# Gate and up projections with the weights as stationary operand, and x normalised before it is transposed

## The chip, the cores and the metric

The kernel runs on one core of a Trainium2 chip. The metric is the device time of one execution in microseconds; the median of several runs is compared. Work is shared by TensorE (PE, matrix products, with PEld for the load of its stationary operand), VectorE (DVE), ScalarE (ACT), GpSimd (POOL) and SyncE (SP), whose queue issues all of the DMAs. The engines run independently and wait for each other through semaphores; each works through its own instructions in order.

## The reference

Two layers of a trunk over 256 tokens of width 1024, in float32. Each layer is a feed-forward block (FFN 1), a mixer and another feed-forward block (FFN 2):

```
def rmsnorm(x, g):
    y = x * lax.rsqrt(jnp.mean(x * x, axis=-1, keepdims=True) + EPS)
    return y * g

def swiglu(h, w_gate, w_up, w_down):            # 1024 -> 2816 -> 1024
    return (jax.nn.silu(h @ w_gate) * (h @ w_up)) @ w_down

for i in range(2):
    x = x + 0.5 * swiglu(rmsnorm(x, ffn1_norm[i]), ...)
    h = rmsnorm(x, mix_norm[i])
    q_s, k_s, v_s, q_m = split(h @ w_in[i])      # 1024 -> 2560
    # layer 0: chunked attention with a relative bias; layer 1: differential attention with
    # rotary positions; both: 4 heads of attention into mem (256 rows, keys and values of its own)
    x = x + concat([o_s, o_m]) @ w_out[i]
    x = x + 0.5 * swiglu(rmsnorm(x, ffn2_norm[i]), ...)
```

## The kernel before

**Number format.** Each operand of a dense product is split into two float32r parts, hi (the value cast) and lo (the rest), and each K tile of 128 rows is three products: hi by hi, hi by lo, lo by hi (`dense`, L375; L382, L385 and L388 are the three). ScalarE makes hi and VectorE makes lo, for activations and for all of the weights.

**Weight stream.** Weights come as chunks of 1 MB ([128, 2048] float32). `loader` issues their DMAs on SP's queue as soon as one of 3 raw buffers is free; `split_hi` (L301) and `split_lo` (L313) split a chunk in four lots of 512 columns into one of 4 pairs of hi and lo buffers. A pair is free again when the last product of its chunk has been issued (`c.uses`). At the start, the loads of x stand between the first chunks on the same queue.

**FFN.** A group is 256 columns of gate and the same 256 of up, two chunks; there are 11 groups (`ffn`, L477). The stationary operand is a K tile of x^T for one block of 128 tokens, the moving operand a [128, 512] piece of weights, gate and up side by side. Per group: 2 token blocks x 8 K tiles x 3 = 48 products of 512 columns into two PSUM banks, one per block. `evac` takes silu of gate (L488) and multiplies by up (L491), for each block. The result h has tokens on its partitions; the down projection needs it with features there, so four transposes per group (L502, issued by `turn`, L395) put h^T into a bank `htp`, and ScalarE and VectorE split it from there (L506, L508). Then the down projection (11 chunks x 8 uses x 3 = 264 products per FFN) adds up in four banks; its last three chunks are worked through block by block and half by half, so that the first token block's x is complete while products of the second still run.

**Normalisation.** `finish` adds a finished half (512 columns of a token block) to x. `prep_half` (L416) at once transposes the raw x (four transposes), multiplies by the norm's gain per column, and splits the result into xh and xl. Squares and the power that gives 1/rms per token (`square`, `prep_rstd`) come later and beside it; 1/rms is applied where the products leave PSUM: as `scale` of the silu and of the multiplication in `evac`, and in the mixer's `head_norm`, `v_evac` and `vq_evac`.

**Order.** The program's order is made by a planner (`Flow`) when the program is built: dense products follow one after another, and the work of the other engines, and transposes, are placed between them by an estimate of when their operands are there, with a fixed cost for each kind (T_MM = 0.216 us for a product of 512 columns). Splits of weights are idle work: they are added when ScalarE's or VectorE's planned queue is under 0.4 us long. At the end of a mixer `table_hint` issues a dummy silu, which loads ScalarE's table for the FFN that follows.

The mixer of layer 0 starts with the products for the memory's keys and values, that of layer 1 with its projection at once (`proj`, L834), block 0 ahead of block 1.

Of the kernel before, what the change touches and what calls it, by code (L numbers as in the profile page):

```python
# [12 lines left out]
F32 = mybir.dt.float32  # L13
F32R = mybir.dt.float32r
# [6 lines left out]
P = 128  # L21
# [19 lines left out]
T_MM = 0.216  # L41
T_TR = 0.107
# [100 lines left out]
def kernel(  # L143
# [44 lines left out]
    load_x(0, 0)  # L188

# [61 lines left out]
    dma_free = [2.3]  # L251
# [10 lines left out]
    def loader():  # L262
        for i, c in enumerate(chunks):
# [4 lines left out]
            for j, (dst, src) in enumerate(c.parts):  # L268
                nc.sync.dma_start(out=dst(c.raw), in_=src)
                dma_free[0] += 2.9 / len(c.parts)  # L270
                if j == 1 and i < 2:
                    c.early = dma_free[0] + LAT
                    if i:
                        load_x(1, 1)
                        dma_free[0] += 0.7
# [61 lines left out]
    def plan_ffn(l, nm, wg, wu, wd):  # L337
        gu = []
        for g in range(NG):
            ids = []  # L340
            for c in range(2):
# [3 lines left out]
                ids.append(add_chunk([q for ab in zip(a, b) for q in ab]))  # L345
# [29 lines left out]
    def dense(ps, xh, xl, ready, c, need, sl, start, stop):  # L375
        """One K tile of a product: three passes over the parts of both operands."""
# [29 lines left out]
    class Xt:  # L406
        def __init__(self):
            self.h = [xtp.tile([P, KT, P], F32R, tag=f"xh{tb}", name=f"xh{tb}") for tb in range(2)]
            self.l = [xtp.tile([P, KT, P], F32R, tag=f"xl{tb}", name=f"xl{tb}") for tb in range(2)]
            self.ss = [sm.tile([P, 2], F32, tag="xss", name="xss", bufs=4) for _ in range(2)]  # L410
            self.r = [sm.tile([P, 1], F32, tag="xr", name="xr", bufs=4) for _ in range(2)]
            self.t = [[None] * KT for _ in range(2)]
            self.rt = [None, None]
            self.done = [0, 0]

    def prep_half(xt, tb, hf, gc, wait=0.0):  # L416
# [12 lines left out]
        nc.scalar.copy(out=xt.h[tb][:, ks, :], in_=y)  # L429
        yield flow.act(512)  # L430
        nc.vector.tensor_sub(xt.l[tb][:, ks, :], y, xt.h[tb].bitcast(F32)[:, ks, :])
# [4 lines left out]
        flow.spawn(square(xt, tb, hf, flow.now + wait))  # L436

    def square(xt, tb, hf, t):
        yield t
        nc.scalar.activation(junk, xs[tb][:, hf * 512:(hf + 1) * 512], AF.Square,  # L440
                             accum_out=xt.ss[tb][:, hf:hf + 1])
        yield flow.act(512, 0.1)
        xt.done[tb] += 1
        if xt.done[tb] == 2:
            yield from prep_rstd(xt, tb)

    def prep_rstd(xt, tb):
        s = small([P, 1], "sst")
        nc.vector.tensor_add(s, xt.ss[tb][:, 0:1], xt.ss[tb][:, 1:2])
        flow.dve(1, 0.15)  # L450
        yield from rsqrt(xt.r[tb], s, 1, 1.0 / D)
        xt.rt[tb] = flow.now
# [6 lines left out]
    def finish(acc, tb, xt, gc, half):  # L459
        for hf in range(2):  # L460
# [12 lines left out]
            else:  # L473
                yield from prep_half(xt, tb, hf, gc)

# [1 line left out]
    def ffn(l, nm, xt, gc_next):  # L477
# [3 lines left out]
        def evac(g, ps, end):  # L481
            hs = []
            for tb in range(2):
                yield lambda: end[tb] is not None and xt.rt[tb] is not None
# [3 lines left out]
                nc.scalar.activation(sil, ps[tb][:, 0:256], AF.Silu, scale=xt.r[tb])  # L488
                yield flow.act(256)
                h = g2.take([P, 256], F32, "h")  # L490
                nc.vector.scalar_tensor_tensor(out=h, in0=ps[tb][:, 256:512], scalar=xt.r[tb], in1=sil,  # L491
                                               op0=ALU.mult, op1=ALU.mult)
                t = flow.dve(256, 0.06)
# [19 lines left out]
        for g, ids in enumerate(plan[l, nm, "gu"]):  # L513
# [4 lines left out]
            order = [(tb, c) for tb in range(2) for c in range(2)] if g == 0 and (l, nm) != (0, 1) else \  # L518
                    [(tb, c) for c in range(2) for tb in range(2)]
            for tb, c in order:  # L520
                for k in range(4):
                    kk = 4 * c + k
                    t = dense(ps[tb], xt.h[tb][:, kk, :], xt.l[tb][:, kk, :], lambda: xt.t[tb][kk], ids[c], k,
                              lambda w: k4(w)[:, k, :], kk == 0, kk == KT - 1)
                if c == 1:
                    end[tb] = t
# [38 lines left out]
    def head_norm(ps, nh, rstd, name):  # L565
        yield g2.has(4)
        sq = g2.take([P, nh * HD], F32, "sq")
        nc.scalar.activation(sq, ps, AF.Square, scale=rstd)
# [8 lines left out]
        nc.vector.scalar_tensor_tensor(out=nat.rearrange("p (h d) -> p h d", d=HD),  # L577
                                       in0=ps.rearrange("p (h d) -> p h d", d=HD), scalar=rstd,
                                       in1=f[:, :nh].unsqueeze(2).broadcast_to([P, nh, HD]),
                                       op0=ALU.mult, op1=ALU.mult)  # L580
# [737 lines left out]
```

## Time and profile before

| what | value |
|---|---|
| runs | 1003.20, 1002.18, 1003.09 us; median 1003.09 |
| span of the profiled execution | 1001.7 us (first to last instruction; the profile gives no time around it) |
| clock granted to TensorE | 1.000 |
| busy: TensorE, VectorE, ScalarE, GpSimd | 991.1, 636.3, 544.5, 58.8 us |
| gate/up products | 2112 (3 x 704) |
| down and output products | 1248 |
| transposes of h | 176 (44 groups of 4) |
| moved by DMA | 177.79 MB, 177 GB/s |

Matrix products overlap in the records (a product's record is about 390 ns long and the next begins before it ends), so their cost is read from the distance between starts. A row of the time order gives the start in us from the span's start, the length in us, the engine, the line, the operation, what it writes and reads, the shape and the count. An arrow in brackets tells how long the engine sat idle before it and what released it.

### The profile page before, as it was taken

To read this page: it belongs to the slowest core of one execution; us is meant where nothing else is said; L and a number is where in the kernel's file an instruction comes from. 1 tells how busy PE (TensorE), PEld (TensorE's weight loads), DVE (VectorE), ACT (ScalarE), POOL (GpSimd) and SP (SyncE) were. 2 spreads that over 40 slices of the span, in tenths; PEclk is the share of its full clock that TensorE was granted. 3 is DMA by queue.
4 is the path that set the end of the run, shared out by engine and by line. 5 is a ranking of instruction groups with operands and counts; after the bars stand their busy time and mean duration, and the time that the engine had idled before them with its cause. 6 is when DMAs were issued, how large, how long until landed. Compare 5 with 4: busy or idle time off the path is not lost.

```text
span 1001.7 us, 13121 instructions
## 1 busy us (share of the span) xinstructions
PE 991.1 (99%) x4772; PEld 817.9 (82%) x4772; DVE 636.3 (64%) x1279; ACT 544.5 (54%) x1159; POOL 58.8 (6%) x65
## 2 busy tenths in 40 slices
PE   8999999999999999999999999999999999999998
PEld 6888888888888888888888888888787888888886
DVE  6756565787666865554466555544989785565542
ACT  6645454776675654554355455444677764554530
POOL 0000000021210000000000000000334100000000
PEclk9999999999999999999999999999999999999999
DMA  8866555575524565655547565555541366655531
GB/s 270 278 189 194 176 202 177 184 253 168 168 85 129 174 202 173 203 171 200 180 126 248 173 203 173 191 188 168 175 162 45 126 210 208 192 186 181 198 126 42
DMA packets 132764, 177.79 MB, mean 177 GB/s; under 512 B 5914, under 2 KB 114011, under 8 KB 132699
## 3 DMA queue, kind: packets, MB, share of 16 engines
q1 hardware_dynamic: 132698, 176.95, 54.9%
q8 instruction: 37, 0.61, 0.2%
q14 instruction: 29, 0.23, 0.1%
HBM read 175.89 MB, written 1.05 MB: 177 GB/s over the span
## 4 chain that ended last, share of the span: by engine, by line
PE 93%; DVE 4%; ACT 1%; DMA 1%; issue 0%; SPq 0%; ACTq 0%
PE gu L382 16%; PE gu L385 16%; PE gu L388 16%; PE acc L385 9%; PE acc L382 9%; PE acc L388 9%; PE pj L388 3%; PE pj L382 2%; PE pj L385 2%; PE htp L395 2%; PE AV L1041 1%; DVE lo L313 1%; PE xtp L395 1%; PE S L973 1%; PE ptp L395 1%; PE kv L388 1%
## 5 line engine op out<-in xcount | busy, mean ns | idle before, releaser
L313 DVE TENSOR_TENSOR lo<-raw,hi 128x512 fp32r<-128x512 f32 x656 | 418.7, 687 | 256.8 <-ACT hi L301 256.5
L301 ACT CAST hi<-raw 128x512 fp32r<-128x512 f32 x656 | 366.0, 618 | 295.6 <-PE gu L388 166.3
L385 PE MATMUL gu<-lo,xh 128*128 128x512 f32 x704 | 277.7, 395 | 0.0
L382 PE MATMUL gu<-hi,xh 128*128 128x512 f32 x704 | 275.0, 391 | 0.0
L388 PE MATMUL gu<-hi,xl 128*128 128x512 f32 x704 | 274.6, 390 | 0.0
L382 PEld LDWEIGHTS gu<-hi,xh 128*128 128x128 f32 x704 | 132.2, 188 | 28.0
L388 PEld LDWEIGHTS gu<-hi,xl 128*128 128x128 f32 x704 | 132.3, 188 | 26.3
L385 PEld LDWEIGHTS gu<-lo,xh 128*128 128x128 f32 x704 | 132.2, 188 | 26.1
L385 PE MATMUL acc<-lo,ht 128*128 128x512 f32 x352 | 137.7, 391 | 0.2 <-DVE lo L313 0.2
L382 PE MATMUL acc<-hi,ht 128*128 128x512 f32 x352 | 137.7, 391 | 0.0
L388 PE MATMUL acc<-hi,ht 128*128 128x512 f32 x352 | 137.5, 391 | 0.0
L385 PEld LDWEIGHTS acc<-lo,ht 128*128 128x128 f32 x352 | 66.1, 188 | 13.9 <-DVE lo L313 0.7
L388 PEld LDWEIGHTS acc<-hi,ht 128*128 128x128 f32 x352 | 66.1, 188 | 13.6
L382 PEld LDWEIGHTS acc<-hi,ht 128*128 128x128 f32 x352 | 66.1, 188 | 13.6
L388 PE MATMUL pj<-hi,xl 128*128 128x512 f32 x160 | 64.4, 403 | 0.0
L385 PE MATMUL pj<-lo,xh 128*128 128x512 f32 x160 | 63.9, 400 | 0.0
L382 PE MATMUL pj<-hi,xh 128*128 128x512 f32 x160 | 63.8, 398 | 0.0
L488 ACT ACTIVATE sil<-gu,xr 128x256 f32<-128x256 f32 x88 | 41.5, 471 | 21.9 <-PE gu L388 21.9
L506 ACT CAST ht<-htp 128x512 fp32r<-128x512 f32 x44 | 25.8, 587 | 37.1 <-PE htp L395 37.1
L491 DVE SCALAR_TENSOR_TENSOR h<-gu,xr,sil 128x256 f32<-128x256 f32 x88 | 42.3, 480 | 2.8
L508 DVE TENSOR_TENSOR ht<-htp,ht 128x512 fp32r<-128x512 f32 x44 | 30.4, 692 | 19.3 <-ACT ht L506 19.3
L402 POOL TENSOR_TENSOR hf<-v,nhalf 128x8 f32<-128x8 f32 (+1 forms) x20 | 30.9, 1546 | 107.3 <-DVE v L400 89.0
(168 smaller groups left out, 835.9 us busy)
## 6 DMA issues: line engine op xcount, KB each, us to landing
raw<-in_ffn_w_down_dram SPq DMA_DIRECT2D x44, 1024.0 KB
raw<-in_ffn_w_gate_dram SPq DMA_DIRECT2D x86, 512.0 KB
raw<-in_ffn_w_up_dram SPq DMA_DIRECT2D x86, 512.0 KB
raw<-in_w_in_dram SPq DMA_DIRECT2D x32, 512.0 KB
raw<-in_w_out_dram SPq DMA_DIRECT2D x8, 1024.0 KB
raw<-in_w_mem_kv_dram SPq DMA_DIRECT2D x4, 1024.0 KB
raw<-in_w_in_dram SPq DMA_DIRECT2D x4, 1024.0 KB
bias<-in_a_rel_bias_dram SPq DMA_DIRECT2D x3, 512.0 KB
```

The costliest lines, as they stand in the source:

```text
L301: nc.scalar.copy(out=c.hi[:, sl], in_=c.raw[:, sl])
L313: nc.vector.tensor_sub(c.lo[:, sl], c.raw[:, sl], c.hi.bitcast(F32)[:, sl])
L382: nc.tensor.matmul(out=ps, lhsT=xh, rhs=wh, start=start, stop=False)
L385: nc.tensor.matmul(out=ps, lhsT=xh, rhs=wl, start=False, stop=False)
L388: nc.tensor.matmul(out=ps, lhsT=xl, rhs=wh, start=False, stop=stop)
L395: nc.tensor.transpose(out=dst, in_=src, identity=flip if flipped else ident)
L402: nc.gpsimd.tensor_tensor(out=dst, in0=v[:, :n], in1=nhalf[:, :n], op=ALU.pow)
L488: nc.scalar.activation(sil, ps[tb][:, 0:256], AF.Silu, scale=xt.r[tb])
L491: nc.vector.scalar_tensor_tensor(out=h, in0=ps[tb][:, 256:512], scalar=xt.r[tb], in1=sil, op0=ALU.mult, op1=ALU.mult)
L506: nc.scalar.copy(out=ht[:, 0], in_=tp)
L508: nc.vector.tensor_sub(ht[:, 1], tp, ht.bitcast(F32)[:, 0])
L973: nc.tensor.matmul(out=ss[e][:, pr, :nk], lhsT=q[rows, pr, :], rhs=k[rows, pr, :], start=i == 0, stop=i == len(passes) - 1)
```

## The change

Four things change, and the planner's figures with them.

- In groups 1 to 10 of each FFN (`held`, `dense_ws`) the operands change places. A [128, 128] piece of the weights is stationary, and x^T of all 256 tokens moves: three products of 256 columns per K tile, for two column halves of gate and then two of up: 4 x 8 x 3 = 96 products per group. The result has features on its partitions, so there are no transposes of h; `evac_ws` works on [128, 512] tiles. Both chunks of a group are now used by all four passes, 16 uses each. Group 0 (`first`) keeps the old form, always one token block after the other.
- xh and xl of both token blocks lie side by side in one tile, so that 256 columns can be read in one product.
- x is multiplied by 1/rms per token (and the constant) ahead of the transposes (`norm_scale`): square of both halves, a sum, the power on GpSimd, two scalings on VectorE, and only then the transposes of both halves. Nothing is scaled any more where products leave PSUM.
- At the start, x's four pieces are loaded in the order block 0, chunk 0, block 1, chunk 1.

```diff
+T_WS = 0.114
 load_x(0, 0)
+load_x(0, 1)
...
-                    if i:
-                        load_x(1, 1)
...
             if i == 0:
                 load_x(1, 0)
-                load_x(0, 1)
+                load_x(1, 1)
...
-                ids.append(add_chunk([q for ab in zip(a, b) for q in ab]))
+                ids.append(add_chunk([q for ab in zip(a, b) for q in ab], 8 if g == 0 else 16))
...
+            self.h = xtp.tile([P, KT, 2, P], F32R, tag="xh", name="xh")
+            self.l = xtp.tile([P, KT, 2, P], F32R, tag="xl", name="xl")
...
+    def square(xt, tb, hf):
+        ss = xt.ss[tb]
+        nc.scalar.activation(junk, xs[tb][:, hf * 512:(hf + 1) * 512], AF.Square, accum_out=ss[:, hf:hf + 1])
+        t = flow.act(512, 0.2)
+        if hf == 0:
+            yield t
+            nc.vector.tensor_scalar(out=ss[:, 2:3], in0=ss[:, 0:1], scalar1=D * EPS, scalar2=None, op0=ALU.add)
+            t = flow.dve(1)
+        return t
+
+    def norm_scale(xt, tb, gc):
+        ss = xt.ss[tb]
+        nc.vector.tensor_add(ss[:, 1:2], ss[:, 1:2], ss[:, 2:3])
+        yield flow.dve(1)
+        nc.gpsimd.tensor_tensor(out=ss[:, 3:4], in0=ss[:, 1:2], in1=nhalf[:, 0:1], op=ALU.pow)
+        yield flow.pool(0.46)
+        yield g2.has(4)
+        for hf in range(2):
+            xn = g2.take([P, 512], F32, "xn")
+            nc.vector.tensor_scalar(out=xn, in0=xs[tb][:, hf * 512:(hf + 1) * 512], scalar1=ss[:, 3:4],
+                                    scalar2=D ** 0.5, op0=ALU.mult, op1=ALU.mult)
+            flow.spawn(prep_half(xt, tb, hf, gc, xn, flow.dve(256)))
...
         for k in range(4):
-            t = turn(tp[:, k, :], xs[tb][:, hf * 512 + k * P:hf * 512 + (k + 1) * P])
+            t = turn(tp[:, k, :], xn[:, k * P:(k + 1) * P])
...
-                yield from prep_half(xt, tb, hf, gc)
+                t = yield from square(xt, tb, hf)
+        if xt is not None:
+            yield t
+            yield from norm_scale(xt, tb, gc)
...
+        def evac_ws(g, gate, up, end):
+            yield lambda: end[0] is not None
+            yield end[0]
+            yield g2.has(3)
+            sil = g2.take([P, 512], F32, "sil")
+            nc.scalar.activation(sil, gate.rearrange("p f t -> p (f t)"), AF.Silu)
+            t = flow.act(512)
+            banks.give()
+            yield t
+            yield lambda: end[1] is not None
+            yield end[1]
+            h = g2.take([P, 512], F32, "h")
+            nc.vector.tensor_tensor(out=h, in0=up.rearrange("p f t -> p (f t)"), in1=sil, op=ALU.mult)
+            t = flow.dve(512)
+            g2.give()
+            banks.give()
+            yield t
+            yield g4.has()
+            ht = g4.take([P, 2, 4, P], F32R, "ht")
+            hi = ht[:, 0].rearrange("p a b -> p (a b)")
+            nc.scalar.copy(out=hi, in_=h)
+            yield flow.act(512)
+            nc.vector.tensor_sub(ht[:, 1].rearrange("p a b -> p (a b)"), h, hi.bitcast(F32))
...
+        def dense_ws(ps, kk, c, k, o, start, stop):
...
+            wh, wl = k4(c.hi)[:, k, o:o + P], k4(c.lo)[:, k, o:o + P]
+            xh, xl = (v[:, kk].rearrange("p a b -> p (a b)") for v in (xt.h, xt.l))
+            nc.tensor.matmul(out=ps, lhsT=wh, rhs=xh, start=start, stop=False)
+            flow.pe(T_WS)
+            nc.tensor.matmul(out=ps, lhsT=wh, rhs=xl, start=False, stop=False)
+            flow.pe(T_WS)
+            flow.step()
+            nc.tensor.matmul(out=ps, lhsT=wl, rhs=xh, start=False, stop=stop)
...
+        def held(g, ids):
+            flow.until(banks.has(2))
+            ps = [bank(n, (P, 2, 256)) for n in ("gate", "up")]
+            end = [None, None]
+            flow.spawn(evac_ws(g, ps[0], ps[1], end))
+            for j in range(2):
+                for f in range(2):
+                    for kk in range(KT):
+                        t = dense_ws(ps[j][:, f, :], kk, ids[kk // 4], kk % 4, j * 256 + f * P, kk == 0, kk == KT - 1)
+                end[j] = t
+
+        for g, ids in enumerate(plan[l, nm, "gu"]):
+            (first if g == 0 else held)(g, ids)
...
-    def start(tb, hf, t):
+    def start(tb, times):
+        for hf in range(2):
+            yield times[hf]
+            t = yield from square(xt, tb, hf)
         yield t
-        yield from prep_half(xt, tb, hf, GC_FFN1, 3.0)
+        yield from norm_scale(xt, tb, GC_FFN1)
...
-        for hf in range(2):
-            flow.spawn(start(tb, hf, (3.75, 8.2, 7.4, 10.4)[2 * tb + hf]))
+        flow.spawn(start(tb, ((4.3, 5.0), (9.6, 10.3))[tb]))
```

In the mixer's `head_norm`, `v_evac` and `vq_evac` the scale 1/rms is dropped (a copy or a plain multiplication stands in its place).

More of the change, by code (lines that the diff above doesn't have):

```diff
@@ L435, in prep_half @@
             xt.t[tb][k] = t
[L436 to L452, printed above, removed]
     class Acc:
@@ L483, in evac @@
             for tb in range(2):
-                yield lambda: end[tb] is not None and xt.rt[tb] is not None
+                yield lambda: end[tb] is not None
                 yield end[tb]
@@ L517, in ffn @@
             flow.spawn(evac(g, ps, end))
[L518 to L526, printed above, removed]
+            for tb in range(2):
+                for c in range(2):
+                    for k in range(4):
+                        kk = 4 * c + k
+                        t = dense(ps[tb], xt.h[:, kk, tb, :], xt.l[:, kk, tb, :], lambda: xt.t[tb][kk], ids[c], k,
+                                  lambda w: k4(w)[:, k, :], kk == 0, kk == KT - 1)
+                end[tb] = t
@@ new lines, in dense_ws @@
+        def dense_ws(ps, kk, c, k, o, start, stop):
+            flow.until(lambda: c.lot[k] is not None and xt.ready(kk) is not None)
+            flow.at(xt.ready(kk))
+            flow.at(c.lot[k])
+            at[0] = max(at[0], c.index)
+            wh, wl = k4(c.hi)[:, k, o:o + P], k4(c.lo)[:, k, o:o + P]
[6 more added lines that the diff above has]
+            nc.tensor.matmul(out=ps, lhsT=wl, rhs=xh, start=False, stop=stop)
+            c.uses -= 1
+            if c.uses == 0:
+                hl_left[0] += 1
+            return flow.pe(T_WS)
@@ L853, in run @@
                 yield t
[L854 to L855 removed]
+                nat = yield from head_norm(ps, 8, None, "qkn")
                 banks.give()
```

56 lines of the change are left out of this document (28 added, 28 removed).

## The prediction

> **What bounds the kernel now.** The page of the profile came first, then the order of time in the gate/up products, in the attention scores, at two stage boundaries and at the start.
>
> ```profile
> span 1001.7 us, 13121 instructions
> PE 991.1 (99%) x4772; PEld 817.9 (82%) x4772; DVE 636.3 (64%) x1279; ACT 544.5 (54%) x1159; POOL 58.8 (6%) x65
> PEclk9999999999999999999999999999999999999999
> GB/s 270 278 189 194 176 202 177 184 253 168 168 85 129 174 202 173 203 171 200 180 126 248 173 203 173 191 188 168 175 162 45 126 210 208 192 186 181 198 126 42
> PE 93%; DVE 4%; ACT 1%; DMA 1%; issue 0%; SPq 0%; ACTq 0%
> L385 PE MATMUL gu<-lo,xh 128*128 128x512 f32 x704 | 277.7, 395 | 0.0
> L506 ACT CAST ht<-htp 128x512 fp32r<-128x512 f32 x44 | 25.8, 587 | 37.1 <-PE htp L395 37.1
> ```
>
> TensorE ends the chain (93%), never idles ahead of a gate/up product (0.0) and has its full clock. So an edit counts for what it does to TensorE's stream. Durations overlap (395 ns for a product); spacing must be read from starts:
>
> ```profile
> 60.41 0.39 PE L388 MATMUL gu<-hi,xl 128*128 128x512 f32 x1
> 61.34 0.39 PE L382 MATMUL gu<-hi,xh 128*128 128x512 f32 x1
> 61.34 0.19 PEld L385 LDWEIGHTS gu<-lo,xh 128*128 128x128 f32 x1
> 63.61 0.39 PE L385 MATMUL gu<-lo,xh 128*128 128x512 f32 x1
> 346.67 0.39 PE L382 MATMUL gu<-hi,xh 128*128 128x512 f32 x1
> 346.90 0.60 PE L395 MATMUL htp<-ident,h 128*128 128x128 f32 x4
> 347.25 0.48 PE L385 MATMUL gu<-lo,xh 128*128 128x512 f32 x1
> 449.14 0.60 PE L395 MATMUL htp<-ident,h 128*128 128x128 f32 x4
> ```
>
> Ten products lie between the starts 61.34 and 63.61: 0.227 us each. Just after a set of transposes (60.41 to 61.34, four products) it is 0.2325. The next weight load starts with the running product (both 61.34) and takes 0.19, so it is hidden. One set of four transposes of h stands in each group (44 sets in all); nine groups lie between 346.90 and 449.14, so a group lasts 11.36 us: 48 x 0.227 = 10.90, and 0.46 for its transposes.
>
> **The change, part by part.** *Groups 1 to 10, four times.* 40 groups x 11.36 = 454.4 us go. In their place stand 40 x 96 = 3840 products of 256 columns, with the weights as stationary operand, and no transposes. All hangs on the spacing of such a product. The only 256-column products are the scores; the second row is a burst that shows the spacing of short ones with a load each:
>
> ```profile
> 299.43 0.75 PE L973 MATMUL S<-km,qmT 64*128 64x256 f32 x10
> 299.78 0.40 PE L973 MATMUL S<-km,qmT 64*128 64x256 f32 x4
> 5.26 1.50 PE L1246 MATMUL warm<-ident 128*128 128x128 f32 x12
> ```
>
> The first two rows are tails of one burst. The scores run side by side in the two row halves of the array, so the six records between 299.43 and 299.78 are three steps in each half: 0.35 / 3 = 0.117 us, each with a load of its own. The warm-up products come every (1.50 - 0.275) / 11 = 0.111 with 275 ns for the last, so a full load fits into 0.111. Bounds: half of 0.227, nothing being fixed per product, is 0.1134 (435.5 us, -18.9); 0.117 plus the 5.5 ns of the disturbed products is 0.123 (472.3, +17.9). I take 0.118, nearest to the scores, with a nanosecond for the full array: 453.1 us, **-1.3**. So the doubled count of products eats nearly all that the transposes give.
>
> The Trainium skill ("TensorE: Matmul & The Clock Gate", Back-to-back issue gap) gives N/2.4 + 2.5 ns: 109.2 for 256 columns, and the sum would be 419.3 us, 35.1 less. By that rule a 512-column product takes 215.8; the trace has 227, so it does not agree and I do not use it.
>
> ```profile
> 522.76 2.49 DVE L313 TENSOR_TENSOR lo<-raw,hi 128x512 fp32r<-128x512 f32 x4
> ```
>
> *ScalarE and VectorE in these groups.* Two silus, two products with up, and a cast and a subtraction from PSUM become one 512-wide instruction of each. TensorE's stream hides them. The splits of the next group's weights get shorter notice: a held group wants all 8 lots in its first 24 products (2.8 us), and its two chunks are given back at its end. VectorE needs 8 x 0.60 = 4.8 us for them (four lots in 2.49, the last 0.69 long: 0.60 apart) inside a group of 11.3, and two chunks of 1 MB per group are 185 GB/s, where the page shows 278 moved. Nothing, then; with that cover gone, each late lot costs 0.25 us.
>
> *Boundary of two FFNs, or of an FFN and mixer 1 (two places).* Today x is transposed when a half is there. Then the second token block's last half went:
>
> ```profile
> 515.55 0.15 DVE L449 TENSOR_TENSOR sst<-xss 128x1 f32<-128x1 f32 x1
> 515.74 0.15 DVE L400 TENSOR_SCALAR v<-sst 128x1 f32<-128x1 f32 x1
> 516.04 0.55 POOL L402 TENSOR_TENSOR xr<-v,nhalf 128x1 f32<-128x1 f32 x1 [175.41 <-DVE v L400]
> 518.92 0.63 ACT L440 ACTIVATE junk<-x 128x512 bf16<-128x512 f32 x1
> 519.09 0.39 PE L388 MATMUL acc<-hi,ht 128*128 128x512 f32 x1
> 519.45 0.19 ACT L440 ACTIVATION_READ_ACCUMULATOR junk<-x 128x1 f32 x1
> 519.76 0.69 DVE L465 SCALAR_TENSOR_TENSOR x<-acc,x 128x512 f32<-128x512 f32 x1
> 521.14 0.60 PE L395 MATMUL xtp<-ident,x 128*128 128x128 f32 x4
> 522.16 0.69 DVE L426 TENSOR_TENSOR y<-xtp,gcol 128x512 f32<-128x512 f32 x1
> 523.18 0.62 ACT L429 CAST xh<-y 128x512 fp32r<-128x512 f32 x1
> 525.17 0.69 DVE L431 TENSOR_TENSOR xl<-y,xh 128x512 fp32r<-128x512 f32 x1
> ```
>
> xl is there at 525.86. After the change the square, the sum, the power and the scaling come in between: 0.63 + 0.19, 0.15, 0.55, and a scaling of 512 elements. That one is not in the trace; the tiny TENSOR_SCALAR (0.15) and the 512-wide two-operand rows (0.69) bound it, I take 0.5. With four gaps between engines at 0.1 (515.74 + 0.15 to 516.04 is 0.15) that is 2.4. The splits queued on VectorE (four behind y at 522.76) will have run by then; I take back 0.7. So xl comes at 527.6, and for the first half too, since both halves now wait for the one square. The second block is wanted 24 products and two sets of transposes after the next product (519.09 + 0.23 + 5.45 + 0.91 = 525.7), its xl in the third product (526.1). Late by **1.5**, twice 3.0. Bounds: bare chain without any queueing, 5.3 of work and eight gaps from 519.5, 525.6, no wait; nothing taken back, 2.2.
>
> *Boundary of a mixer and its second FFN (two places).* Here a token block has only 24 products (5.45 us) after it.
>
> ```profile
> 327.70 0.68 DVE L468 TENSOR_TENSOR x<-acc,x 128x512 f32<-128x512 f32 x1
> 330.03 0.69 DVE L426 TENSOR_TENSOR y<-xtp,gcol 128x512 f32<-128x512 f32 x1
> 330.76 0.63 ACT L429 CAST xh<-y 128x512 fp32r<-128x512 f32 x1 [3.08 <-DVE y L426]
> 331.64 0.68 DVE L431 TENSOR_TENSOR xl<-y,xh 128x512 fp32r<-128x512 f32 x1
> 332.57 0.39 PE L382 MATMUL gu<-hi,xh 128*128 128x512 f32 x1
> 333.21 1.28 ACT L561 ACT_TABLE_LOAD   x1
> 334.51 0.20 ACT L561 ACTIVATE dummy<-dummy 128x1 f32<-128x1 f32 x1
> ```
>
> The first block's x is complete at 328.38. With 2.0 for square, sum, power and scaling, 0.6 for the transposes, 0.69 for y and six gaps of 0.1, xh starts at 332.3, is done at 333.0, xl at 333.7. The FFN starts at 332.57 and wants xl at 333.0: 0.7 late at best. But the table load is issued at the end of the projection; if xh falls in behind it on ScalarE's queue, xh starts at 334.7 and xl is there at 336.1: 3.1 late. I take **2.0**, twice 4.0. Behind the waiting product stands all of TensorE's queue, the second block's transposes too. That block's chain gains the same 2.0 of notice, which covers it. Mixer 0 has the memory's keys and values ahead of its own products (96 x 0.227 = 21.8 us) and waits for nothing.
>
> *Start.* SP's queue now has both halves of the first x block ahead of chunk 0, and both of the second ahead of chunk 1; before, x(0,1) came after chunk 0 and x(1,1) inside chunk 1. The bytes up to the end of chunk 1 are the same.
>
> ```profile
> 10.37 0.66 PE L395 MATMUL xtp<-ident,x 128*128 128x128 f32 x4 [3.60 <-DMA x<-in_x_dram]
> 10.78 0.48 PE L382 MATMUL gu<-hi,xh 128*128 128x512 f32 x1
> 14.82 0.62 ACT L301 CAST hi<-raw 128x512 fp32r<-128x512 f32 x1 [0.53 <-DMA raw<-in_ffn_w_up_dram]
> ```
>
> Today the first product (10.78) waits behind transposes of a later block (10.37). The normalised chain of block 0, begun with x(0,1) a microsecond after x(0,0) (0.26 MB at 270 GB/s), ends about there as well. But chunk 1, whose second part lands at 14.8, is wanted after 12 products instead of 24. Its third and fourth lots end near 16.1 and 16.7, the 24th product near 17.5; today it would be 10.78 + 5.45 + 0.9 = 17.1. So **+0.5**, between -0.5 and 2.
>
> *Sum.* -1.3 + 3.0 + 4.0 + 0.5 = +6.2 on the span of 1001.7: 1007.9. The runs' median, 1003.09, is 1.4 above the span, so 1009.3.
>
> **Rivals.** (a) *The chain is hidden.* The bare chain at the FFN boundary is just in time (525.6 for 526.1), and the splits queued in its way could run later. Then only 1.4 at the mixers is left: -1.3 + 1.4 + 0.5, 1003.7. Against it: VectorE had no idle time around 522 to 526.
> (b) *Faster: half the columns, half the time.* If a product has no fixed part, it takes 0.1134, the groups lose 18.9 and the waits of 7.5 give it back in part: 991.7. It decides from 0.1163 on, where 3840 x (0.1183 - T) pays for 7.5. For it: a load fits into 0.111. Against it: 0.117 in the scores. The quoted rule's 109.2 is its far end, 975.5.
> (c) *Fixed cost of short products.* At 0.123, 17.9 + 7.5: 1028.5. The 0.2325 after transposes shows such a part, steady stretches do not.
> (d) *Loads no longer hidden.* If a load waits for the product before it, a step is 0.111 + 0.1134, 3840 of them 862 us: 1418. The scores' loads in one row half, 0.117 apart, speak against it. The Trainium skill (same page, The mechanism, on packing) has loads overlap running products only when their row groups differ; by that rule (d) would hold, but the trace does not agree, with 61.34 for a load and the product of the same rows.
> (e) *Splits late.* One microsecond in half the groups: 1029.
>
> **How the numbers follow.** Forecast 0.52 (its own range 1002 to 1018), (a) 0.14, (b) 0.18 with its far end at 0.03, (c) 0.12, (d) 0.02, (e) 0.02. Changes under 0.2%, 2 us, are about what a measurement of this kernel can't tell from none: from 1001.1 to 1005.1. Faster: (b) and 0.02 of (a), 0.20. Same: the rest of (a) and 0.08 of the forecast, 0.20. Slower: 0.60. The range 994 to 1023 holds the forecast, (a), and the inner halves of (b) and (c).
>
> **What would show it.** Starts of gate and up products 0.118 apart, held groups of 11.3 us; TensorE idle ahead of the first FFN product after a mixer, released by xh or xl, and ahead of the second block's products elsewhere. A spacing under 0.116 or over 0.120, or boundaries without idle time, would make the forecast wrong.

## The result, and the profile after

The changed kernel took 1029.63 us (median of four runs, 1027.37 to 1032.79), the kernel before beside it 1003.14: a ratio of 1.0266, 95% interval 1.0244 to 1.0289. It is slower, as forecast, but by 26.5 us where 6.2 were forecast, and 1029.63 lies above the range. On another chip the same pair gave 1029.32 against 1002.17 (1.0260). In what follows, *before* and *after* name the two kernels.

From the page of the profile after (span, busy shares, granted clock in 40 slices, shares of the chain, one group of new products):

```profile
span 1031.0 us, 16610 instructions
PE 1009.9 (98%) x6532; PEld 910.4 (88%) x6532; DVE 630.0 (61%) x1263; ACT 526.9 (51%) x1119; POOL 61.6 (6%) x65
PEclk8999999999999999999999999999899999999999
PE 91%; DVE 6%; ACT 2%; issue 1%; DMA 0%; POOL 0%; SPq 0%; ACTq 0%; DVEq 0%
L578 PE MATMUL gate<-xh,lo 128*128 128x256 f32 x640 | 181.5, 284 | 0.0
```

TensorE still ends the chain, but its share fell from 93% to 91% and VectorE's rose from 4% to 6%. The clock row has an 8 in the first slice and another in slice 29, where the page of before shows only nines. A new product never waits (0.0). So two questions follow: what a new product costs, and what happens between the stages.

The profiled execution of after, the slowest of its four (1032.79 us), is 29.3 us longer than that of before. With the starts of products from the time order, that splits as follows. "Group 0" is the distance from the first product of an FFN to the first of its group 1.

| part | forecast | in the profile | from |
|---|---|---|---|
| groups 1 to 10, four FFNs | -1.3 | +6.2 | gate/up behind group 0 +8.0; transposes of group 10 gone, 4 x 0.46 |
| start to the first product of group 1 | +0.5 | +5.3 | 22.70 before, 27.99 after |
| FFN to FFN | +1.5 | +4.9 | group 0 11.35 and 16.79; 0.5 of it are transposes moved here from the stage before |
| mixer 0 and the FFN after it | +2.0 | +3.5 | 1.2 ahead of the FFN, 2.4 in its group 0, 0.4 in the keys and values, 0.5 moved out |
| mixer 1 and the FFN after it | +3.5 | +9.4 | mixer 7.2, group 0 2.7, 0.5 moved out |
| sum | +6.2 | +29.3 | |

The spacing of the new products, from the time order of TensorE in a held group:

```profile
599.81 0.28 PE L575 MATMUL up<-xl,hi 128*128 128x256 f32 x1
601.01 0.28 PE L578 MATMUL up<-xh,lo 128*128 128x256 f32 x1
```

Ten products lie between the two starts: 0.120 us each, and over every undisturbed pass of 48 it is the same. A group is 96 x 0.120 = 11.52 us, against 11.36 with its transposes.

The place where the prediction had its main row, FFN to FFN, in the time order of all engines after (start, length, engine, line; in brackets the idle time before and who ended it):

```profile
530.40 0.39 PE L387 MATMUL acc<-hi,ht 128*128 128x512 f32 x1
530.83 0.69 DVE L474 SCALAR_TENSOR_TENSOR x<-acc,x 128x512 f32<-128x512 f32 x1 [0.17 <-PE acc L387]
531.44 2.49 DVE L312 TENSOR_TENSOR lo<-raw,hi 128x512 fp32r<-128x512 f32 x4
531.76 0.63 ACT L418 ACTIVATE junk<-x 128x512 bf16<-128x512 f32 x1
533.84 0.15 DVE L429 TENSOR_TENSOR xss<-xss 128x1 f32<-128x1 f32 x1
533.91 1.89 DVE L312 TENSOR_TENSOR lo<-raw,hi 128x512 fp32r<-128x512 f32 x3
534.08 2.14 POOL L431 TENSOR_TENSOR xss<-xss,nhalf 128x1 f32<-128x1 f32 x1 [9.97 <-DVE xss L429]
536.25 0.88 DVE L436 TENSOR_SCALAR xn<-x,xss 128x512 f32<-128x512 f32 x2 [0.45 <-POOL xss L431]
536.88 1.06 PE L394 MATMUL xtp<-ident,xn 128*128 128x128 f32 x8 [0.65 <-DVE xn L436]
537.55 1.29 DVE L452 TENSOR_TENSOR y<-xtp,gcol 128x512 f32<-128x512 f32 x2
538.27 1.22 ACT L455 CAST xh<-y 128x512 fp32r<-128x512 f32 x2 [1.62 <-DVE y L452]
538.94 0.50 PE L381 MATMUL gu<-hi,xh 128*128 128x512 f32 x1 [1.00 <-ACT xh L455]
539.95 1.28 DVE L457 TENSOR_TENSOR xl<-y,xh 128x512 fp32r<-128x512 f32 x2
540.69 0.50 PE L387 MATMUL gu<-hi,xl 128*128 128x512 f32 x1 [1.02 <-DVE xl L457]
```

Before, xl's record began 5.4 us after x's (519.76 to 525.17); now it is 9.1 (530.83 to 539.95), and the product that uses it starts at 9.9. Of these, four splits of weights stand between x and the sum on VectorE (531.44, 2.49 us), three more run beside the power, and the power of 128 numbers on GpSimd takes 2.14 us where the row of before has 0.55. TensorE waits three times, 0.65 + 1.00 + 1.02. (These are idle times behind the end of a record; from start to start each wait takes about 0.2 longer, 3.2 us in all.)

And then a thing no step of the prediction had. The next two fences are of after: first TensorE's rows just behind these waits, then stretches of the span (columns: from and to, length, busy time of each engine with its instructions, granted clock, DMA share, GB/s).

```profile
543.03 0.63 PE L381 MATMUL gu<-hi,xh 128*128 128x512 f32 x1
543.46 0.63 PE L384 MATMUL gu<-lo,xh 128*128 128x512 f32 x1
```

```profile
541.50:544.90 3.40, 3.40 (x10) 2.64 (x9) 0.34 (x1) 0.35 (x1) 0.00 (x0) 0.52 0.51 137
545.20:548.00 2.80, 2.80 (x16) 2.38 (x15) 2.50 (x4) 1.87 (x4) 0.00 (x0) 1.00 0.49 166
723.80:740.00 16.20, 13.45 (x50) 10.13 (x49) 14.53 (x26) 8.11 (x17) 4.69 (x4) 0.79 0.55 177
9.00:28.00 19.00, 17.28 (x65) 13.73 (x66) 17.11 (x33) 13.16 (x27) 0.98 (x1) 0.73 0.80 248
```

After the waits the granted clock falls to 0.52 for some 3 us, and products stand 0.43 us apart instead of 0.227. It happens behind three of the four boundaries' waits (here, at the entry of mixer 1 and behind it) and at the start, 30 products in all; in the execution of before none does without a wait between. At the entry of mixer 1 (the third row) TensorE is idle 2.75 of 16.20 us and the mean clock is 0.79. Its waits there are 1.67 and 0.96 us, 3.0 from start to start, and eleven slow products add 2.2, so that place alone loses 5.2.

Mixer 0 to its FFN, in the time order of after:

```profile
338.43 1.28 ACT L631 ACT_TABLE_LOAD   x1
339.83 1.12 ACT L455 CAST xh<-y 128x512 fp32r<-128x512 f32 x2
340.48 0.50 PE L381 MATMUL gu<-hi,xh 128*128 128x512 f32 x1 [1.56 <-ACT xh L455]
```

xh fell in behind the table load on ScalarE's queue, as the prediction feared; TensorE stands 1.56 us ahead of the product that uses it.

### The profile page after: what moved, and what is told of

Same layout as the page of the kernel before. It is cut to its first block, busy times and chain, and to the rows that moved or that the text cites. A ratio compares the mean times of both kernels' runs of the same rounds, so it can differ in the third digit from the quotient of the medians.

```text
span 1031.0 us, 16610 instructions
## 1 busy us (share of the span) xinstructions
PE 1009.9 (98%) x6532; PEld 910.4 (88%) x6532; DVE 630.0 (61%) x1263; ACT 526.9 (51%) x1119; POOL 61.6 (6%) x65
## 4 chain that ended last, share of the span: by engine, by line
PE 91%; DVE 6%; ACT 2%; issue 1%; DMA 0%; POOL 0%; SPq 0%; ACTq 0%; DVEq 0%
PE acc L384 9%; PE acc L381 9%; PE acc L387 9%; PE gate L578 7%; PE up L578 7%; PE up L575 7%; PE up L573 7%; PE gate L575 7%; PE gate L573 7%; PE pj L387 3%; PE pj L381 3%; PE pj L384 3%; DVE lo L312 2%; PE AV L1111 1%; PE gu L387 1%; PE gu L381 1%
## 5 line engine op out<-in xcount | busy, mean ns | idle before, releaser
L578 PE MATMUL gate<-xh,lo 128*128 128x256 f32 x640 | 181.5, 284 | 0.0
L573 PE MATMUL gate<-xh,hi 128*128 128x256 f32 x640 | 181.2, 283 | 0.0
L573 PE MATMUL up<-xh,hi 128*128 128x256 f32 x640 | 181.1, 283 | 0.0
L575 PE MATMUL up<-xl,hi 128*128 128x256 f32 x640 | 181.1, 283 | 0.0
L578 PE MATMUL up<-xh,lo 128*128 128x256 f32 x640 | 181.1, 283 | 0.0
L575 PE MATMUL gate<-xl,hi 128*128 128x256 f32 x640 | 181.1, 283 | 0.0
L573 PEld LDWEIGHTS gate<-xh,hi 128*128 128x128 f32 x640 | 122.8, 192 | 0.2
L573 PEld LDWEIGHTS up<-xh,hi 128*128 128x128 f32 x640 | 122.9, 192 | 0.0
L575 PEld LDWEIGHTS up<-xl,hi 128*128 128x128 f32 x640 | 122.9, 192 | 0.0
L578 PEld LDWEIGHTS up<-xh,lo 128*128 128x128 f32 x640 | 122.9, 192 | 0.0
```

Of the source, the lines that this page charges most:

```text
L573: nc.tensor.matmul(out=ps, lhsT=wh, rhs=xh, start=start, stop=False)
L575: nc.tensor.matmul(out=ps, lhsT=wh, rhs=xl, start=False, stop=False)
L578: nc.tensor.matmul(out=ps, lhsT=wl, rhs=xh, start=False, stop=stop)
```

## The experiments

### Each half of the change alone

The first run keeps the new products but transposes raw x as soon as a half is there. The second keeps the normalisation ahead of the transposes, but all groups in the old form.

```diff
# held groups, x raw
-                t = yield from square(xt, tb, hf)
+                flow.spawn(prep_half(xt, tb, hf, gc, xs[tb][:, sl], flow.now))
-            yield t
-            yield from norm_scale(xt, tb, gc)
```

> The changed kernel without the normalisation: x is transposed raw as soon as a half is there; squares, power and scaling by 1/rms are left out. Theory (products cost 0.120 us, all the rest of the loss is the normalisation in the way at the stage boundaries): 40 groups x 96 x 0.120 = 460.8 us for 454.4, and a start about as before: 1003.1 + 6.4 = 1009 to 1011. Rival (the held groups themselves upset the boundaries, because both chunks are given back only at a group's end and splits come late): 1020 or more, with TensorE still idle at the boundaries.

```diff
# normalised first, old groups (8 uses of a chunk)
-            (first if g == 0 else held)(g, ids)
+            first(g, ids)
```

> The changed kernel with groups 1 to 10 in the old form (x stationary, 512 columns, transposes of h); x is still normalised ahead of its transposes. Theory: the boundaries lose as in the changed kernel, the groups last 11.36 us again: 1029.6 - 6.4 = 1023. Rival (held groups upset the boundaries): 1003 to 1008, boundaries without idle time.

Measured: 1013.55 us (1.0112, 1.0097 to 1.0127), 11.6 above the kernel before; and 1022.53 us (1.0206, 1.0179 to 1.0233), 20.5 above. So the normalisation, with the order that it forces, costs about twice what the held groups cost. The two sum to 32.1, more than the 26.5 to 27.2 of the whole: both carry the new order of x's loads, and each has a planned order of its own, so the halves can be ranked but not added. The profile of the first is 9.8 us longer than that of before, which comes from another chip. The four FFNs' held groups are +6.5 us of it (+6.2 in after); the 3.3 left over lie in the stage of keys and values (+1.6) and in mixer 1 (+1.7), where the planner placed other work. That this placing is the cause is argued, not shown.

### Is it the width of a product, or which operand is held?

The kernel before, with x^T stationary as ever, and only the products of groups 1 to 10 cut into two of 256 columns, or four of 128:

```diff
+                for i in range(CUT):                       # CUT = 2, CUT = 4
+                    o = slice(i * 512 // CUT, (i + 1) * 512 // CUT)
+                    for kk in range(KT):
+                        t = dense(ps[tb][:, o], ..., lambda w: k4(w)[:, kk % 4, o], kk == 0, kk == KT - 1, CUT)
```

> The kernel before, with each 512-column product of groups 1 to 10 cut into two of 256 columns; x stays stationary, transposes stay. Theory (a fixed 13 ns per product, whichever operand is stationary): 3840 x 0.120 = 460.8 us for 1920 x 0.2267 = 435.3, 1003.1 + 25.5 = 1028.6. Rival (0.120 comes from freshly split weights being loaded as stationary operand, and halves of the old form cost half): 1003 to 1005.

> As the one before, cut into four of 128 columns. Theory of a fixed cost alone: 7680 products of 0.0667 us, 512 us for 435.3: 1080. Rival (the load of 128 columns of weights is a floor of 0.111 per product, which 256 columns just clear): 852 us, 1420.

Measured: 1026.7 us (1.0241, 1.0219 to 1.0262) with two, 1422.1 with four (one run). The time order of TensorE, two rows of each, the first pair seven products apart, the second fourteen:

```profile
599.75 0.28 PE L389 MATMUL gu<-hi,xl 128*128 128x256 f32 x1
600.59 0.28 PE L383 MATMUL gu<-hi,xh 128*128 128x256 f32 x1
```

```profile
799.80 0.27 PE L389 MATMUL gu<-hi,xl 128*128 128x128 f32 x1
801.36 0.28 PE L386 MATMUL gu<-lo,xh 128*128 128x128 f32 x1
```

0.84 / 7 = 0.120 and 1.56 / 14 = 0.111. With 0.120, 40 x (96 x 0.120 + 0.46) = 479.2 us stand against 454.4: 24.8, and 24.7 were measured. So a 256-column product costs 0.120 whichever operand is held; that the weights are stationary has no price of its own. With four, 40 x (192 x 0.111 + 0.46) = 870.9 would be +416.5, and +420.1 was measured. The forecast of a fixed part alone (1080) fell: a product shorter than about 0.111 us gains nothing, and the warm-up rows of the prediction had that spacing. That the load of the stationary operand, which each product brings, sets this floor is argued from it, not shown by itself.

### The power on GpSimd

In after, the power is replaced by a reciprocal on VectorE, with no root, so that the stretched GpSimd instruction and the hop to it are gone.

```diff
-        nc.gpsimd.tensor_tensor(out=ss[:, 3:4], in0=ss[:, 1:2], in1=nhalf[:, 0:1], op=ALU.pow)
+        nc.vector.reciprocal(out=ss[:, 3:4], in_=ss[:, 1:2])
```

> The changed kernel with the power on GpSimd replaced by a reciprocal on VectorE: the root is left out, so x is scaled by 1/sum instead of 1/rms. Theory (GpSimd's step is stretched by VectorE's work, 2.14 us at the boundary of the two FFNs where 0.55 was forecast, and lies on the waiting chain): 5 to 7 us less, 1023 to 1025. Rival (the chain is held up by the splits queued on VectorE, and a shorter step only moves the wait): 1028 or more.

Measured: 1028.62 us (1.0264, 1.0248 to 1.0280): nothing gained. The theory of that run fell. The time order of its VectorE shows why:

```profile
533.38 0.15 DVE L429 TENSOR_TENSOR xss<-xss 128x1 f32<-128x1 f32 x1
533.45 0.68 DVE L312 TENSOR_TENSOR lo<-raw,hi 128x512 fp32r<-128x512 f32 x1
534.05 0.15 DVE L431 RECIPROCAL xss<-xss 128x1 f32<-128x1 f32 x1
534.12 0.67 DVE L312 TENSOR_TENSOR lo<-raw,hi 128x512 fp32r<-128x512 f32 x1
534.72 0.88 DVE L436 TENSOR_SCALAR xn<-x,xss 128x512 f32<-128x512 f32 x2
```

A split now slips in ahead of the reciprocal and another ahead of the scaling. The step itself takes 0.15 us, but from sum to scaling it is still 1.34, because every step put on VectorE's queue can be preceded by a split. In after the same two steps lie 2.41 apart (533.84 to 536.25), in a second execution of it (below) 1.87. Against that one half a microsecond is gained here and gone again further down: from x to the first waiting product both take 7.6 us.

### The splits kept out of the way

In after, while a block is being normalised, splits of chunks further on than the next are held back (ScalarE's and VectorE's alike).

```diff
-                yield lambda: flow.free["V"] <= flow.now + SLACK or i <= at[0] + AHEAD
+                yield lambda: (flow.free["V"] <= flow.now + SLACK and (not chain[0] or i <= at[0] + 1)) or i <= at[0] + AHEAD
...
+            if hf and xt is not None:
+                chain[0] += 2
```

> The changed kernel; from the moment a token block's x is complete until its xl is there, splits of chunks beyond the next one are not queued on ScalarE and VectorE. Theory (the splits stretch the chain, directly and through GpSimd): 6 to 10 us less, 1020 to 1024, GpSimd's power back near 0.55 to 0.9. Rival (the bare chain of ten steps is too long in any case): 1027 or more; splits that come late after it would show as idle time released by lo in group 1.

Measured: 1021.57 us (1.0199, 1.0185 to 1.0213), 7.8 below the changed kernel's 1029.32, and the intervals don't touch. (The two ran on different chips, on which the kernel before took 1002.05 and 1002.17.) The same boundary, in its time order (TensorE, VectorE, GpSimd):

```profile
526.26 0.69 DVE L476 SCALAR_TENSOR_TENSOR x<-acc,x 128x512 f32<-128x512 f32 x1 [0.79 <-PE acc L388]
528.67 0.15 DVE L430 TENSOR_TENSOR xss<-xss 128x1 f32<-128x1 f32 x1
528.90 0.93 POOL L432 TENSOR_TENSOR xss<-xss,nhalf 128x1 f32<-128x1 f32 x1 [9.37 <-DVE xss L430]
529.94 0.88 DVE L437 TENSOR_SCALAR xn<-x,xss 128x512 f32<-128x512 f32 x2
533.54 0.50 PE L382 MATMUL gu<-hi,xh 128*128 128x512 f32 x1 [0.98 <-ACT xh L456]
534.79 0.50 PE L388 MATMUL gu<-hi,xl 128*128 128x512 f32 x1 [0.52 <-DVE xl L458]
```

x to scaling is 3.7 us instead of 5.4, x to the waiting product's xl 8.5 instead of 9.9. Part of the splits still run there, since the next chunk's can't wait.

### The steps of the normalisation left out

The calm kernel, in which square, sum and power are left out too and x is scaled by a constant; scaling, transposes and all else stay.

```diff
-            nc.vector.tensor_scalar(out=xn, in0=..., scalar1=ss[:, 3:4], scalar2=D ** 0.5, ...)
+            nc.vector.tensor_scalar(out=xn, in0=..., scalar1=D ** -0.5, scalar2=D ** 0.5 / 8, ...)
```

> The calm version with square, sum and power left out: x is scaled by a constant, in the same place, ahead of the transposes of both halves. Theory (what is left of the boundaries' loss once the splits are held back is the length of the chain, about 2.4 us of these three steps and their gaps): the waits at the four boundaries all but vanish, 1015 to 1017, near the 1013.6 of the version without any normalisation. Rival (the loss is that both halves wait for the last one, or that splits come late): 1020 or more.

Measured: 1010.62 us (1.0083, 1.0060 to 1.0106), 11.0 below the calm kernel and lower than either theory had it. At the FFN boundary the transposes now stand behind twelve of the first block's products (in after behind all 24), and no product waits:

```profile
524.41 1.04 PE L395 MATMUL xtp<-ident,xn 128*128 128x128 f32 x8
525.20 0.47 PE L382 MATMUL gu<-hi,xh 128*128 128x512 f32 x1
```

The lengths of the parts, from starts of products in the profiles (us):

| | before | after | after, second profile | calm | calm, steps left out |
|---|---|---|---|---|---|
| start to group 1 | 22.70 | 27.99 | 27.70 | 25.49 | 22.52 |
| group 0, FFN 2 of layer 0 | 11.37 | 13.76 | 13.74 | 12.74 | 11.78 |
| group 0, FFN 1 of layer 1 | 11.35 | 16.79 | 14.67 | 13.86 | 11.81 |
| group 0, FFN 2 of layer 1 | 11.48 | 14.21 | 14.15 | 12.80 | 11.81 |

In the last column each group 0 is that of before plus the 0.46 us of a moved set of transposes, give or take 0.13, and the start is back. So all that is lost in these four places is the lateness of square, sum and power, with the splits in their way and the clock behind it. That both halves of x wait for the last one, the rival, costs nothing here: it is so in this version too. Of the 27.2 us between the changed kernel (1029.32) and the kernel before it (1002.17), 7.8 go to the splits in the way, 11.0 to the three steps once these splits are gone, and 8.4 stay, of which 6.2 are the held groups.

### The clock

The changed kernel once more, unaltered, on the chip of the version with the steps left out (above) and of the combination at the end of this part:

> The changed kernel again, unaltered, for a comparison on one chip with the two others here: 1027 to 1031.

Measured: 1029.32 us (1.0260, 1.0235 to 1.0284). Its FFN boundary, TensorE's two waiting rows and the stretch around them:

```profile
538.12 0.50 PE L381 MATMUL gu<-hi,xh 128*128 128x512 f32 x1 [1.00 <-ACT xh L455]
539.87 0.50 PE L387 MATMUL gu<-hi,xl 128*128 128x512 f32 x1 [1.01 <-DVE xl L457]
```

```profile
523.00:548.00 25.00, 22.87 (x120) 18.85 (x119) 20.60 (x38) 15.07 (x30) 1.48 (x2) 1.00 0.43 135
```

The clock stayed at 1.00, and group 0 is 14.67 instead of 16.79. Two of the three waits are the same to a hundredth; the one of 0.65 ahead of the transposes is missing. So of the 2.1 us between the profiles, 0.5 are that wait (1.03 us from the product before to the transposes in the first profile, 0.50 here) and 1.6 are the clock (6.73 and 5.14 us from the product that waits for xl to group 1). The kernel with normalisation first and old groups has all three waits (0.65, 0.99, 1.02) and still products 0.227 us apart behind them, so the length of the waits alone doesn't settle whether the clock falls.

What does is where they lie in time. In each execution the clock changes on a fixed grid of 3.41 us: in after's clock record, half-clock stretches begin at 541.66, 732.81 and 838.62 us, 56 and 31 times 3.413 apart, and last 3.41, 6.83 and 3.41 us. Here are two grid stretches of after, then two of the second profile:

```profile
538.25:541.66 3.41, 1.70 (x6) 1.14 (x7) 3.41 (x6) 1.22 (x2) 0.00 (x0) 1.00 0.70 229
541.66:545.08 3.42, 3.42 (x9) 2.65 (x9) 0.18 (x1) 0.53 (x2) 0.00 (x0) 0.50 0.56 157
534.69:538.10 3.41, 2.31 (x14) 1.56 (x12) 3.32 (x8) 1.65 (x5) 0.02 (x1) 1.00 1.07 362
538.10:541.51 3.41, 2.38 (x9) 1.68 (x10) 2.92 (x5) 0.56 (x1) 0.00 (x0) 1.00 0.63 206
```

In after, TensorE was idle 1.71 of the 3.41 us, and the next stretch ran at half clock. In the second profile the grid cuts between the two waits, 1.10 and 1.03 idle, and nothing fell. With all thirteen profiles cut this way, each of the 29 stretches at full clock with 1.7 us or more of idle time is followed by one at half clock (ends of executions, and the idle time before the first product, included), and none with less than 1.6; of three with 1.62 or 1.63, one is.

The power took 0.93 there, not 2.14, and the scaling still started 4.9 after x (530.53 to 535.42), not 5.4: half a microsecond is all that the stretched power cost.

Then idle products, which nobody reads, put in front of the waiting products at the four boundaries (not at the start):

```diff
+    def fill(n):
+        b = bank("fill")
+        for _ in range(n):
+            nc.tensor.matmul(out=b[:, 0, :], lhsT=ident, rhs=ident, start=True, stop=True)
...
+        if n:
+            fill(n)                                        # n = 4, ahead of the first and the third product
```

> The changed kernel with idle products on the identity (4 float32 products, about 0.9 us) ahead of the first and the third product of the waiting token block at four boundaries. Theory (after the waits TensorE's clock is halved for some 3 us, 24 products of 512 columns then 0.427 apart, 5 us in all, and activity keeps it up): granted clock 0.997 or more, 3 to 5 us less, 1025 to 1027. Rival (the clock does not depend on the idle time, or the products themselves delay the path): 1029 to 1032.

Measured: 1026.99 us (1.0249, 1.0235 to 1.0263). That is 2.6 less than after's first median and 2.3 less than its second, short of the 3 to 5 expected, and the intervals overlap; the granted clock of the execution rose from 0.991 to 0.998, with three slow products left. The fill is in its time order, in place of an idle stretch (each of its four products shows as two):

```profile
535.10 1.06 PE L378 MATMUL fill<-ident 128*128 128x128 f32 x8
536.83 1.05 PE L378 MATMUL fill<-ident 128*128 128x128 f32 x8
```

So by the medians the clock's share is two to three microseconds, not clear of noise; in the first profile of after the 30 slow products, 0.2 us too long each, make 6. Calm, fill and longer warm-up together:

```diff
# calm and fill as above, the start's first block too
-    warm(6)
+    warm(20)
```

> The changed kernel with the held-back splits of the calm version, the idle products of the filled version (now also at the start) and 14 more warm-up products at the start. Theory (contention and the halved clock are separate losses, and the start loses some 2 us to the clock): the calm version's 1021.6 less 1.5 for its slow products at the boundaries and 2 at the start, 1017 to 1019, granted clock 0.999 or more. Rival (once the waits are short the clock costs nothing, and idle products only get in the way): 1021 to 1024.

Measured: 1021.95 us (1.0191, 1.0167 to 1.0215), with a clock of 1.000 from end to end, and no better than the calm kernel alone (1.0199). Its start to group 1 is 25.72 us, the calm kernel's 25.49. So the theory of that run fell. It seems that, once the splits are out of the way, the full clock only lets TensorE arrive earlier at data that isn't there; that the idle products themselves take back what the clock gives isn't ruled out.

### The order of x's loads

The kernel before, with only the order of x's four loads changed as in after (and the planner's times for them):

```diff
     load_x(0, 0)
+    load_x(0, 1)
...
-                load_x(0, 1)
+                load_x(1, 1)
```

> The kernel before with the changed kernel's order of x loads alone (both halves of block 0 ahead of chunk 0, both of block 1 ahead of chunk 1). Theory (the first product starts 3 us sooner, as without normalisation, but the weights' arrival takes most of it back): 0 to 1.5 us less, 1000.5 to 1002. Rival (the weights' arrival alone sets the end of group 0): no change; if chunk 1 is late, up to 1 us more.

Measured: 1003.91 us (1.0021, 1.0012 to 1.0031), 1.9 above; a gain of up to 1.5 was expected. Its start, in the time order of TensorE:

```profile
8.18 0.50 PE L380 MATMUL gu<-hi,xh 128*128 128x512 f32 x1 [0.17 <-ACT hi L299]
14.13 0.50 PE L380 MATMUL gu<-hi,xh 128*128 128x512 f32 x1 [1.52 <-ACT xh L427]
```

The first product starts at 8.18 instead of 10.78, but TensorE then idles 1.5 us for the second block's xh, and group 1 begins at 22.73, as before (22.70). Where the 1.9 us are lost is open: its profiled span, 1001.6, is that of before, 1001.7, but before's was taken on another chip, and on this one its runs have a median near 1002.

## Why the prediction was right or wrong

The direction held, and so did the outline of the mechanism: the doubled number of products eats the gain of the transposes, and normalising ahead of the transposes makes the next stage wait. The size failed, 6.2 against 26.5 us, and with it what the prediction had of the chain at the boundaries and at the start.

**Groups 1 to 10 (-1.3).** The mis-sized term is T: 0.118 forecast, 0.120 measured. Two nanoseconds times 3840 are the 7.7 us that turn -1.3 into +6.4 (6.2 by the stages). The scores, 0.117 apart, were the wrong neighbour: they hold only 64 rows and run side by side in two halves (that this is why they differ is argued). Two rows of this kernel would now give it: 0.2267 at 512 columns and 0.120 at 256 are, by a straight line, 0.417 ns per column and 13.3 ns per product, and it is these 13.3 ns that the change pays twice. Rival (b), half the columns in half the time, fell: the spacing is above the 0.1163 where it would begin. Rival (c) named the right kind of cost, but at 0.123; that its 1028.5 is near the measured time is chance, for in it the groups lose 17.9. Rival (d), loads not hidden, fell; there is a floor for a product with its load, but at 0.111.

The Trainium skill ("TensorE: Matmul & The Clock Gate", Back-to-back issue gap) gave N/2.4 + 2.5 ns, 109.2 for such a product; the section calls that the gap of an isolated product and names about 131 ns at 512 columns for a stream of loads and products. The trace keeps the formula's slope and not its fixed part, 120.0 here and 226.7 at 512 columns, and does not agree with the 131.

**Splits, ScalarE and VectorE inside the groups (0).** Right: every undisturbed pass of 48 is 0.120 apart, with no product waiting for a split. Rival (e) fell: splits hurt, but not there; that its 1029 is near the measured time is chance too.

**The boundaries (3.0 + 4.0) are the step that failed:** +17.8 us in the profile (4.9 + 3.5 + 9.4). Worst are the two places put at 1.5 each. From start to start, TensorE waits 3.2 us at the FFN boundary and 3.0 at the entry of mixer 1, and the slow clock behind adds 1.6 and 2.2. The chain was costed at 7.8 us from x to xl; it is 9.8 in after to the end of the first half's xl, whose record begins at 539.95. What was wrong in it, and what was missing:

- *"I take back 0.7", for splits that will have run by then.* The opposite holds: four stand between x and the sum, three more ahead of the scaling, and where a step moved to VectorE, a split went in ahead of it. Keeping the later chunks' splits away is worth 7.8 us over the kernel.
- *0.55 for the power.* It took 2.14, and 0.93 in the second profile; of these 1.2 us only 0.5 show on the path, and the run without the power gained nothing. The 0.5 for a scaling was right (two in 0.88).
- *Both halves wait for the one square.* The prediction named this and took no cost for it. All steps of both halves do lie one behind the other now (eight transposes, two y, two xh, two xl), but with the three steps left out they still do, and no product waits for them.
- *Missing: the clock.* The prediction let a microsecond of waiting cost a microsecond. In after, 2.7 us of waits within five brought products at half speed for three more; that is 1.6 us at the FFN boundary by comparison of two profiles.

Between a mixer and its FFN (2.0 each) the step held as put: xh fell in behind the table load, and by the starts TensorE waits 2.9 us at mixer 0 and 2.4 at mixer 1, for the first block's xh and xl. The second block's chain gained the notice that the prediction gave it: no product of it waits as much as 0.1 us. That group 0 is 2.4 and 2.7 us longer there is the first block's wait for xl, the transposes moved in and, at mixer 1, six slow products.

**The start (0.5).** It lost 5.3. That chain was put down as ending "about there as well"; it is normalisation once more, for with the steps left out the start is 22.52. The order of the loads by itself doesn't move group 1.

**Chances.** Slower had 0.6, rightly. The range ended at 1023, between the forecast's own upper end (1018) and rival (c); each boundary's upper bound (2.2, 3.1) left out contention, which the row quoted for it, four splits in 2.49 us, was showing.

## What to carry to other kernels

When a product is made shorter, measure the fixed part per product first, at two widths of the same kind of product with the same rows in use; multiplied by thousands, a nanosecond decides. When a step that ran beside the work is put into a chain, cost the chain with everything that can stand in its engines' queues, idle work included, and not with bare durations; here a scheduling rule that kept idle work away took back 7.8 us. And a wait of TensorE may cost more than its length, if waits add up to half of one of the clock's stretches.

## What the runs showed of the hardware

- A float32r product with a load of its own costs 0.417 ns per column and 13.3 ns beside it, by the line through 0.2267 at 512 columns and 0.120 at 256 (the latter with either operand held), down to a floor near 0.111 us, which the product of 128 columns shows.
- The granted clock fell to half (0.50; products 0.43 us apart) for stretches of 3.41 us, on a grid of that length that is fixed within an execution. It fell behind grid stretches in which TensorE was idle for 1.7 us or more in total, never behind one with less than 1.6, however the waits were cut up. The Trainium skill ("TensorE: Matmul & The Clock Gate", What's actually happening) puts the fall behind at least one idle window of about 3.4 us and lets that window run free of the kernel. The second agrees with the traces: most of the same two waits fell into one stretch in after (1.71 us idle), and each into one of its own in the second profile (1.10 and 1.03). With the first they do not agree, since half a stretch was enough; no single wait at the three boundaries where after's clock fell is longer than 1.7 us.
- One power of 128 numbers on GpSimd took 0.55 to 2.14 us, by this row of the changed kernel (shortest, median, longest in ns, and when). The longest ran while VectorE was subtracting back to back (533.91); that the two contend is argued from that overlap, and wasn't tried by itself.

```profile
L431 POOL TENSOR_TENSOR xss<-xss,nhalf x12: 550/712/2137, 5.8 to 838.7; 128x1 f32<-128x1 f32 x12
```
